# First MLP product: the weight sums behind both additions from PSUM, the low parts later, and a root one product later

## The chip, the cores and the metric

The kernel runs on one core of one Trainium2 chip. Its engines work side by side, each on its own queue of instructions: TensorE (PE in the profile; PEld are its weight loads) multiplies, VectorE (DVE), ScalarE (ACT) and GpSimd (POOL) do the rest, and SyncE (SP) starts transfers (DMA). They wait for one another through semaphores. SBUF is the memory that all engines work on, PSUM the banks that TensorE writes its products to. The metric is the time of one execution on the device in microseconds (us), less is better.

## The reference

Two sequences of 512 rows and 1024 columns go through two layers, a Fourier mixer with an MLP and an attention with an MLP:

```python
def sq_relu_mlp(h, w_up, w_down):
    a = jnp.maximum(h @ w_up, 0)
    return (a * a) @ w_down

def trunk(x, ...):
    for i in range(DEPTH):
        ...
        x = x + sq_relu_mlp(rms_norm(x, mlp_norm[i]), mlp_w_up[i], mlp_w_down[i])
    return rms_norm(x, final_norm)
```

`w_up` is 1024 x 4096 and `w_down` 4096 x 1024. Only `h @ w_up` of both layers, its squared ReLU, and the norm ahead of it bear on the change; the Fourier mixer, the attention and the second product are the same before and after.

## The kernel before

**Numbers.** Everything is float32. [...] A product is three matmuls for each 128 rows of depth: high by high, high by low, low by high. `halves` splits a 128 x 1024 tile and gives its two halves of 512 columns.

**The first MLP product** is one step of the Strassen-Winograd scheme over blocks: seven block products instead of eight. `h`, transposed and normed, gives four blocks, by depth (first or second 512) and by sequence (0 or 1); out of them `Blocks` makes b11, b21 (sequence 0), b12, b22 (sequence 1) and the sums t1 to t4. A `Pair` is two neighbouring tiles of 128 columns of `w_up`, of 512 KB each: `raw` holds a11 and a12 (the two halves of the depth), `r1` holds a21 and a22. From these VectorE makes four sums:

- `sums_23`, three instructions (L862, L863, L864): s3 = a11 - a21, then s1 = a21 + a22 in the place of a21, then s2 = s1 - a11. s2 and s3 share a tile `s` of the raw pool.
- `sum_4`: x4 = a12 - s2.

Then `split_23`, `split_1` and `split_4` make high and low parts: s2 and s3 with one cast and one subtraction of 1024 columns, s1 and a22 likewise, and x4 with 512 columns.

**The order in a pair.** `product` (L812) issues the 12 matmuls of one block product. `first` (b11) and `second` (b21) are the products of `raw`; `rest` does the other five in the order t2, t3, t1, t4, b22. In each layer the first pairs (`AHEADS`: 8 in layer 0, 6 in layer 1) have `first` and `second` done in a loop of their own, since they need sequence 0 alone, and are called early here; the later ones (`late`) have `first` ahead of `rest` and `second` within it, so that they have seven products and the early ones five. Layer 0 has 16 pairs, layer 1 has 14 and four tiles that are multiplied in the plain way (`Regular`).

`rest` accumulates in three banks, `ob`, `oc` and `od`, and VectorE adds their results:

- L885: u2 = t2's bank + b11's product, behind t2
- L889: u3 = bank `oc` + u2, behind t3. t4 goes on accumulating into `oc`, so its first matmul waits for this addition
- L900: u3 = bank `od` + u3, behind t1, then ReLU and square on ScalarE (`squares`, L827 and L828). b22 goes on accumulating into `od`, so it waits for this one
- L907: v = bank `oc` + u2, behind t4, then squares
- L914: bank `od` + u2, behind b22, then squares

Behind `rest`, `out` makes four subtractions on GpSimd (L922 to L925) for the second MLP product and seven transfers of the results to memory. While pair p is multiplied, the sums and the splits of pair p+1 (`nxt`) are made: they stand between the additions. The weights of pair p+2 are loaded behind `rest` of pair p (SP's queue).

**What sets the order.** In `rest` of the early pairs VectorE's order is the one that is written down (`manual_schedule` for DVE); the other engines' order there, and every order elsewhere, is found by the scheduler of the framework, which starts from the written order. `rest` of the last pair has VectorE's and SP's order by hand, and in layer 0 TensorE's too.

**The root.** The norm needs the inverse root of the mean square of each row of `x`. ScalarE squares the 8 tiles of a sequence (L157), GpSimd adds them up (L159), TensorE sums the columns (L165, 8 small matmuls by ones), and `rsqrt` makes the root with small instructions of VectorE and one or two of ScalarE. `spread` lets TensorE transpose the result to every partition (L173) and ScalarE copy it (L174). `Blocks.second` then norms sequence 1 (L212) and makes its blocks and sums, a part behind each of the early pairs from p = 4 on. `root(1)` is issued in the loop of the early pairs, behind `second` of p = 2, and `spread(1)` ahead of p = 3 in layer 0 and behind `second` of p = 3 in layer 1.

## Time and profile before

| | us |
|---|---|
| median of 3 runs | 1739.89 |
| lowest and highest | 1738.68, 1741.07 |
| the profiled execution, its own time | 1740.44 |
| its span, first to last instruction | 1738.6 |
| mean granted clock of TensorE | 0.992 |

The profile is one execution. Its stages, by stretches of the span with the busy time of TensorE in each:

| stretch, us | what runs there | TensorE busy, us |
|---|---|---|
| 0 to 160 | Fourier mixer, b11 and b21 of layer 0's early pairs | 130.82 |
| 160 to 290 | rest of the early pairs of layer 0 | 126.74 |
| 290 to 450 | late pairs of layer 0 | 159.46 |
| 450 to 870 | second product of layer 0 and the head of layer 1 | 414.47 |
| 870 to 1160 | rest of the attention, b11 and b21 of layer 1's early pairs | 287.32 |
| 1160 to 1260 | rest of the early pairs of layer 1 | 98.45 |
| 1260 to 1410 | late pairs of layer 1 | 150.00 |
| 1410 to 1738 | plain tiles, second product of layer 1, final norm | 318.07 |

The boundaries are rounded, so that a stretch holds a little of its neighbour. How to read it: a matmul's busy time runs to a modelled end and the next one overlaps it, so an idle time in a row is smaller than what the wait costs. A row of the timeline reads: start in us, length, engine, line, operation, output and inputs with their shapes, the number of instructions that the row stands for, and in brackets the idle time ahead of it with what ended it.

### The profile page before, as it was taken

Reading aid. Unit: us, or ns where it says so; the run is one execution under the profiler, and the core shown is the slowest. Engines: PE = TensorE matmul, PEld = TensorE weight load, DVE = VectorE, ACT = ScalarE, POOL = GpSimd, SP = SyncE. Lnnn points to the kernel's source line nnn. Section 1 sums busy time; section 2 is a strip of 40 time slices with the busy share of each in tenths; the row PEclk is TensorE's granted clock in tenths of the full one; section 3 lists DMA queues with packets and bytes.
Section 4 is the critical chain, followed back from the end, with each engine's and each line's share of the span. In section 5 each row is a group of like instructions: output and inputs, shape, how many; then the busy total and the mean of one; then the engine's idle time right before and its main releaser. Section 6 shows DMA issues by size and latency. Waiting matters only on the chain. (4 is left out here: it accounts for less than half of the span.)

```text
span 1738.6 us, 21980 instructions
## 1 busy us (share of the span) xinstructions
PE 1685.3 (97%) x7870; PEld 1396.4 (80%) x7870; DVE 1250.9 (72%) x1855; ACT 871.2 (50%) x1530; POOL 349.8 (20%) x308
## 2 busy tenths in 40 slices
PE   4999999999999999999999999999999999999997
PEld 4887788888788888788877888787788878888886
DVE  8768776555878879975578843697745479787865
ACT  6666444545433434546687724554544554344334
POOL 3330444222000000412234302104332200000004
PEclk9999999999999999999999999999999999999999
DMA  9823455448754545420100213225544487455322
GB/s 281 234 93 121 159 195 192 152 182 286 277 180 159 194 144 195 156 106 25 49 25 1 97 49 120 90 101 188 199 157 151 172 313 265 147 207 186 127 74 97
DMA packets 103893, 267.11 MB, mean 154 GB/s; under 512 B 10200, under 2 KB 10200, under 8 KB 103784
## 3 DMA queue, kind: packets, MB, share of 16 engines
q1 hardware_dynamic: 87624, 233.73, 37.5%
q10 hardware_dynamic: 14112, 25.70, 3.9%
q0 software_dynamic: 2048, 6.29, 1.9%
q8 instruction: 61, 1.00, 0.2%
q14 instruction: 48, 0.39, 0.1%
HBM read 190.70 MB, written 73.92 MB: 152 GB/s over the span
## 5 line engine op out<-in xcount | busy, mean ns | idle before, releaser
L812 PE MATMUL ps<-u,w 128*128 128x512 f32 x4704 | 1083.9, 391 | 9.5 <-DVE w L83 5.0
L812 PEld LDWEIGHTS ps<-u,w 128*128 128x128 f32 x4704 | 882.5, 188 | 202.7 <-DVE t L889 7.8
L82 ACT CAST w<-raw 128x1024 fp32r<-128x1024 f32 (+1 forms) x226 | 219.6, 982 | 428.2 <-PE ps L812 268.4
L83 DVE TENSOR_TENSOR w<-raw,w 128x1024 fp32r<-128x1024 f32 (+1 forms) x226 | 260.1, 1153 | 54.7 <-ACT w L82 54.3
L159 POOL TENSOR_TENSOR t<-t,t 128x512 f32<-128x512 f32 (+1 forms) x56 | 80.2, 1436 | 734.1 <-ACT t L157 678.5
L83 DVE TENSOR_TENSOR u<-u,u 128x1024 fp32r<-128x1024 f32 x133 | 163.0, 1254 | 23.9 <-ACT u L82 23.9
L82 ACT CAST u<-u 128x1024 fp32r<-128x1024 f32 x133 | 133.3, 1043 | 72.7 <-PE ps L812 47.5
L77 PE MATMUL ps<-u,u 128*128 128x512 f32 (+2 forms) x424 | 162.6, 385 | 1.7 <-DVE u L604 0.9
L78 PE MATMUL ps<-u,u 128*128 128x512 f32 (+2 forms) x424 | 157.6, 372 | 5.7 <-DVE u L83 5.6
L79 PE MATMUL ps<-u,u 128*128 128x512 f32 (+2 forms) x424 | 157.9, 372 | 2.0 <-POOL u L83 1.5
L1059 DVE TENSOR_TENSOR u<-ps,u 128x512 f32<-128x512 f32 x160 | 109.8, 689 | 57.1 <-PE ps L812 56.1
L812 PE MATMUL ps<-u,u 128*128 128x512 f32 x528 | 126.9, 390 | 2.6 <-DVE t L900 1.8
L922 POOL TENSOR_TENSOR u<-u 128x512 f32<-128x512 f32 x28 | 36.1, 1289 | 414.9 <-ACT u L828 414.9
L812 PEld LDWEIGHTS ps<-u,u 128*128 128x128 f32 x528 | 98.6, 188 | 25.5 <-issue 2.9
L78 PEld LDWEIGHTS ps<-u,u 128*128 128x128 f32 x424 | 82.9, 195 | 18.0 <-DVE u L83 7.8
L79 PEld LDWEIGHTS ps<-u,u 128*128 128x128 f32 x424 | 82.5, 195 | 15.9 <-POOL u L83 2.1
L77 PEld LDWEIGHTS ps<-u,u 128*128 128x128 f32 x424 | 83.0, 196 | 13.8 <-ACT u L82 1.8
L83 DVE TENSOR_TENSOR u<-ps,u 128x512 fp32r<-128x512 f32 (+4 forms) x126 | 76.5, 627 | 17.8 <-ACT u L82 16.5
L885 DVE TENSOR_TENSOR t<-ps,u 128x512 f32<-128x512 f32 x30 | 20.8, 692 | 91.4 <-PE ps L812 89.9
L82 ACT CAST u<-ps 128x512 fp32r<-128x512 f32 (+4 forms) x126 | 66.5, 542 | 24.9 <-PE ps L79 14.2
L795 DVE TENSOR_TENSOR u<-ps,u 128x512 f32<-128x512 f32 (+1 forms) x48 | 30.9, 645 | 64.7 <-PE ps L79 64.7
L827 ACT ACTIVATE t<-t 128x512 f32<-128x512 f32 x60 | 37.8, 631 | 56.1 <-DVE t L900 45.4
(225 smaller groups left out, 2007.8 us busy)
## 6 DMA issues: line engine op xcount, KB each, us to landing
raw<-w_up SPq DMA_DIRECT2D x82, 512.0 KB, 3.9
u<-spill_t SPq DMA_DIRECT2D x60, 512.0 KB, 6.0
raw<-w_sum SPq DMA_DIRECT2D x56, 512.0 KB, 3.7
u<-spill_b SPq DMA_DIRECT2D x45, 512.0 KB, 5.6
spill_t<-u SPq DMA_DIRECT2D x87, 256.0 KB, 2.0
spill_b<-t ACTq DMA_DIRECT2D x60, 256.0 KB, 2.0
raw<-w_row SPq DMA_DIRECT2D x28, 512.0 KB, 3.5
park<-u SPq DMA_DIRECT2D x24, 512.0 KB, 3.2
```

The costliest lines, as they stand in the source:

```text
L77: nc.tensor.matmul(out, lh, rh, start=first, stop=False)
L78: nc.tensor.matmul(out, lh, rl, start=False, stop=False)
L79: nc.tensor.matmul(out, ll, rh, start=False, stop=last)
L82: nc.scalar.copy(dst_hi, src)
L83: eng.tensor_sub(dst_lo, src, f32(dst_hi))
L159: nc.gpsimd.tensor_add(acc[q][:, :n], acc[q][:, :n], s[:, :n])
L795: nc.vector.tensor_add(x[:, :n], o[:, :n], x[:, :n])
L812: nc.tensor.matmul(o, w[x][:, sl], h[k][y], start=first and k + i == 0, stop=k == n - 1 and i == 2, skip_group_check=not first)
L827: nc.scalar.activation(t, src, AF.Relu)
L885: nc.vector.tensor_add(u2, ob, t[:, 0])
L922: eng.tensor_sub(t[:, 0], b12, b11)
L1059: nc.vector.tensor_add(x, o, x)
```

## The change

In `rest`, three things move in the written order, in both layers and all pairs but the last:

- `sums_23` of the next pair goes from between L885 and t3 to behind L889 (pair 0 had it there already).
- `split_23` goes from behind L889 to behind L900 and its squares.
- `sum_4` and `split_1` go from ahead of `v` to behind `v` and its squares.

In layer 0 alone (there `2 * np_ == NF`) two things move in the loop of the early pairs: `root(1)` from behind `second` of pair 2 to between `first` and `second` of pair 3, and `spread(1)` from ahead of pair 3 to ahead of pair 4. No instruction is added or removed. Behind the change the lines of `rest` from the second addition on stand two lower: L887 for L889, L896 for L900, and L920 to L923 for L922 to L925.

```diff
                 u2, u3, t = tm(), tm(), self.t
                 product(ob, self.s2, b("t2"))
                 nc.vector.tensor_add(u2, ob, t[:, 0])
-                if nxt and self.p > 0:
-                    nxt.sums_23()
                 product(oc, self.s3, b("t3"))
                 nc.vector.tensor_add(u3, oc, u2)
                 if self.late:
                     self.second()
                 if nxt:
-                    if self.p == 0:
-                        nxt.sums_23()
-                    nxt.split_23()
+                    nxt.sums_23()
                 if nxt and nxt.p >= ah:
                     nxt.split_row()
                 next(fill, None)
                 product(od, self.s1, b("t1"))
                 nc.vector.tensor_add(u3, od, u3)
                 squares(u3, u3)
+                if nxt:
+                    nxt.split_23()
                 product(oc, self.a22, b("t4"), False)
-                if nxt:
-                    nxt.sum_4()
-                    nxt.split_1()
                 next(fill, None)
                 v = tm()
                 nc.vector.tensor_add(v, oc, u2)
                 squares(v, v)
+                if nxt:
+                    nxt.sum_4()
+                    nxt.split_1()
                 next(fill, None)
                 if nxt:
                     nxt.split_4()
...
         for p in range(ah):
-            if 2 * np_ == NF and p == 3:
+            if 2 * np_ == NF and p == 4:
                 blocks.spread(1)
...
             pair.first()
+            if 2 * np_ == NF and p == 3:
+                blocks.root(1)
             if p > 0:
                 pair.second()
             if p == 1:
                 pairs[0].second()
-            if p == 2:
+            if p == 2 and 2 * np_ < NF:
                 blocks.root(1)
```

## The prediction

> **What bounds the kernel now.** I read the page first: its span, and the share of it that each engine is busy.

> ```profile
> span 1738.6 us, 21980 instructions
> PE 1685.3 (97%) x7870; PEld 1396.4 (80%) x7870; DVE 1250.9 (72%) x1855; ACT 871.2 (50%) x1530; POOL 349.8 (20%) x308
> raw<-w_up SPq DMA_DIRECT2D x82, 512.0 KB, 3.9
> ```

> TensorE is busy 97% of the span, and the change removes no matmul. So it can only shorten or lengthen TensorE's waits. The waits of TensorE by releaser (total, times, longest) say which of them the edited lines can reach.

> ```profile
> PE ps L812 <- DVE t L889: 2.8, 2, 1.9
> PE ps L165 <- POOL t L159: 2.6, 3, 1.5
> PE ps L812 <- DVE t L900: 1.8, 3, 0.6
> ```

> L889 is the second addition from PSUM in `rest`, L900 the third, L165 the column sums in `root`. These totals are too small: a gap counts only past the modelled end of a matmul. TensorE's timeline shows what hides. I take the third to fifth pair of layer 0; the rows of 12 are the last product of a pair (b22), the rows of 48 the next pair's first four.

> ```profile
> 190.24 2.88 PE L812 MATMUL ps<-u,u 128*128 128x512 f32 x12
> 204.07 2.88 PE L812 MATMUL ps<-u,u 128*128 128x512 f32 x12
> 206.79 11.34 PE L812 MATMUL ps<-u,w 128*128 128x512 f32 x48
> 217.96 2.88 PE L812 MATMUL ps<-u,u 128*128 128x512 f32 x12
> ```

> A product of 12 takes 206.79 - 204.07 = 2.72 us, 0.227 per matmul, so five take 13.61; but a pair takes 217.96 - 204.07 = 13.89. The missing 0.28 us is a short wait in every pair, before t4, which accumulates onto the bank that L889 reads. VectorE, GpSimd (POOL) and ScalarE in such a pair, whose t2 starts at 206.79:

> ```profile
> 206.99 0.69 DVE L914 TENSOR_TENSOR u<-ps,t 128x512 f32<-128x512 f32 x1 [0.49 <-PE ps L812]
> 209.77 0.69 DVE L885 TENSOR_TENSOR t<-ps,u 128x512 f32<-128x512 f32 x1 [2.08 <-PE ps L812]
> 210.37 0.68 DVE L862 TENSOR_TENSOR raw<-raw,raw 128x512 f32<-128x512 f32 x1
> 211.09 1.67 DVE L863 TENSOR_TENSOR raw<-raw 128x512 f32<-128x512 f32 x1
> 212.79 1.66 DVE L864 TENSOR_TENSOR raw<-raw,raw 128x512 f32<-128x512 f32 x1
> 214.38 0.68 DVE L889 TENSOR_TENSOR t<-ps,t 128x512 f32<-128x512 f32 x1
> 215.62 1.23 DVE L83 TENSOR_TENSOR w<-raw,w 128x1024 fp32r<-128x1024 f32 x1 [0.57 <-ACT w L82]
> 209.14 1.29 POOL L922 TENSOR_TENSOR u<-u 128x512 f32<-128x512 f32 x1 [7.42 <-ACT u L828]
> 210.51 1.70 POOL L923 TENSOR_TENSOR u<-t,u 128x512 f32<-128x512 f32 x1
> 212.17 1.73 POOL L924 TENSOR_TENSOR u<-t,u 128x512 f32<-128x512 f32 x1
> 213.87 1.74 POOL L925 TENSOR_TENSOR t<-t,u 128x512 f32<-128x512 f32 x1
> 214.54 2.00 ACT L82 CAST w<-raw 128x1024 fp32r<-128x1024 f32 x2 [5.53 <-DVE raw L864]
> ```

> The sums L863 and L864 take 1.67 instead of 0.69 us: each ends 0.55 after a POOL subtraction ends, and each subtraction ends 1.15 after a sum. Two-operand instructions on SBUF of these engines take turns. L889, which reads PSUM, takes 0.68 beside a running POOL. It is late because it stands behind the sums.

> **The change, part 1: sums behind both additions.** No instruction is added. Three sums (L862 to L864) go behind the second addition, which then ends at 5.44 + 0.26 + 0.69 = 6.39 us from the pair's start (an addition starts 0.26 behind its product: 209.77 against 206.79 + 2.72), before t4 at 8.16. The wait of 0.28 goes, but something else is late: the third addition now stands behind the sums, and b22 waits for it at 10.89.

> Let POOL start its four subtractions at 3.94. They run 3.94 to 5.23 and 5.31 to 6.60. L862, ready at 6.31, ends 0.55 later, at 7.15; the third subtraction at 8.30, L863 at 8.85, the fourth at 10.00, L864 at 10.55. The third addition runs 10.46 to 11.15 (successive starts overlap by 0.09, as 209.77 + 0.69 and 210.37 show), and b22 starts at 11.21 instead of 10.89: 0.32, and 0.11 for the weight load restarting, together 0.43 us.

> Then the cast runs 10.64 to 11.69 (0.09 behind L864, two of them 2.00) and the low part to 12.94, before the next t2 needs it at 14.04. v's addition starts at 12.85, the fourth sum 13.45, the low part of the raw pair 14.06, that of x4 15.23, and t0's addition 15.84 to 16.53. L914 ended at 207.68 and POOL began at 209.14, two squares and 1.46 later; so POOL starts at 17.99, which is 3.95 in the next pair of 14.04. The ring closes: **0.43 against 0.28 now.** Where ScalarE makes the square of v before the cast of x4 (in the changed order the first three pairs of layer 0), POOL starts 0.2 later and the wait is 0.52 + 0.11 = 0.63.

> The first pairs and the last one ahead of the long ones have their own rows.

> ```profile
> 171.33 2.20 PE L812 MATMUL ps<-u,w 128*128 128x512 f32 x9
> 174.28 2.36 PE L812 MATMUL ps<-u,w 128*128 128x512 f32 x9 [0.75 <-ACT w L82]
> 187.38 2.79 PE L812 MATMUL ps<-u,w 128*128 128x512 f32 x11 [1.89 <-DVE t L889]
> 274.29 0.93 PE L812 MATMUL ps<-u,u 128*128 128x512 f32 x3 [0.61 <-DVE t L900]
> 1175.54 1.66 PE L812 MATMUL ps<-u,w 128*128 128x512 f32 x6 [0.94 <-DVE t L889]
> 172.46 0.69 DVE L864 TENSOR_TENSOR raw<-raw,raw 128x512 f32<-128x512 f32 x1
> ```

> To each bracket 0.16 is added, because a matmul's record lasts 0.39 while the next is due after 0.227, and some 0.1 for the restart. Pair 0 of layer 0 loses 0.75 + 0.16 + 0.11 = 1.02, pair 1 loses 1.89 + 0.16 + 0.11 = 2.16, pair 7 loses 0.85; with six short waits layer 0 loses 1.02 + 2.16 + 6 x 0.28 + 0.85 = 5.7. Layer 1: 1.21 + 4 x 0.28 + 0.85 = 3.2. Of pair 0's nine matmuls from 174.28, all belong to pair 1 and cover part of a wait; the changed order puts b22 of pair 0 first.

> After: in pair 0 I hang VectorE's order on the product ends; L864 ends about 173.7 (now 173.15, because the second addition waits for t3 ahead of a low part), b22 is due at 173.37 and waits for the addition that ends at 174.3: 1.0 + 0.11. POOL then starts at 4.2 in pair 1. Pairs 1 to 3 cost 0.63 each, 4 to 6 0.43. In pair 7 the low part of the next row stands ahead of the third addition too: one cast more on ScalarE in pair 6 puts POOL at 4.43, L864 ends at 11.0, the low part after the last subtraction at 12.2, the addition at 12.8, b22 waits 1.95 + 0.11 = 2.06. Layer 0: 1.1 + 1.9 + 1.3 + 2.1 = 6.4. Layer 1 starts with POOL at 2.6 and no wait in three pairs, then 0.53, 0.43 and 2.06: 3.0. **Part 1: 9.4 - 8.9 = +0.5 us.**

> Bounds: below, if the sums never meet POOL, only pair 0 waits, and 9.4 falls to 1.1, a gain of 7.8. Above, if all three sums wait a whole turn (1.67 each, as L863), the third addition ends at 11.95 and b22 waits 1.23 in each pair: 11 pairs x 1.23 and twice 2.9 make 20.4 with pair 0's 1.1, a loss of 11.5. I take the ring, because it closes on the rows' own durations.

> **What moves at no cost.** The low parts go behind the squares: the next t2 needs them at 14.04 and they end at 12.94, a cover of 1.1 us. The raw buffers come free some 2 us later, so two loads per pair start later on SP; they land in 3.9 us and are needed 6.3 us into the next pair but one. The long pairs (seven products, 19.05 us) have the final addition at about 12.85 against b22 at 13.6: no wait, as now.

> **Part 2: the root of sequence 1.** It issues column sums on TensorE, five small VectorE and two ScalarE instructions, no DMA; its spread four transposes and a copy.

> ```profile
> 120.79 1.09 PE L812 MATMUL ps<-u,w 128*128 128x512 f32 x4
> 123.40 1.26 PE L165 MATMUL ps<-ones,t 128*128 128x2 f32 x8 [1.52 <-POOL t L159]
> 121.61 1.03 ACT L82 CAST w<-raw 128x1024 fp32r<-128x1024 f32 x1
> 120.69:124.10 3.41, 1.19 (x6) 0.62 (x4) 1.00 0.69 275
> 124.10:127.52 3.42, 3.00 (x7) 2.49 (x8) 0.50 0.00 0
> 185.55:188.96 3.41, 1.58 (x7) 1.32 (x8) 1.00 0.42 162
> 135.52 4.63 DVE L212 TENSOR_TENSOR u<-u,t 128x1024 f32<-128x1024 f32 x4 [0.43 <-ACT t L174]
> 142.85 1.23 DVE L83 TENSOR_TENSOR w<-raw,w 128x1024 fp32r<-128x1024 f32 x1 [1.57 <-ACT w L82]
> ```

> TensorE waits 1.52 us for the last square's addition on POOL. The last three rows with a colon are windows of L812 alone (TensorE's busy time, its loads', the granted clock, DMA): behind a window with 1.19 us of full matmuls in 3.41 (35%) the clock is 0.50 for 3.42 us; behind one with 1.58 (46%) it stays at 1.00. At half clock seven matmuls take 3.0 us, 1.4 to 1.5 more than at full clock.

> In the changed order only two matmuls of pair 3 come ahead of the sums. They need the cast that ends at 122.64, run 122.7 to 123.15, and the sums start at 123.40 as now. That is 0.45 us of work inside the wait. It also lifts the window to 1.64 us (48%), above the one that kept its clock. **Part 2: -0.45 - 1.49 = -1.9 us.** Bounds: 0, if the cast is late, and -2.0. The norms (L212) move behind one more low part; VectorE is idle for 1.57 before 142.85, so this is covered; without the cover it costs 1.2.

> [...]

> **Sum.** The profiled execution took 1740.44 us for its span of 1738.6. 1740.44 + 0.5 - 1.9 = **1739.0 us**; the median of the runs is 1739.89, 0.55 lower than the profiled one. I hold to the former.

> **Rivals.**
> A, no meeting: if POOL starts at 2.6 to 3.3 in every pair, as at the head of layer 1, the waits of pairs 1 to 6 and of layer 1 fall away (1.9 + 1.3 + 1.0) and the two long ones to today's 0.85 (2.4): 1739.0 - 6.6 = 1732.4. For it: the ring has slack of 0.3 only. Against: low parts now stand ahead of t0's addition, and 15.84 against today's 14.1 follows from fixed durations.
> B, slower, the ring slips: if POOL starts past 4.9, the three sums meet three subtractions. One mechanism, at b22: 1.23 us in nine pairs (six of layer 0, three of layer 1) instead of 3.2 + 1.0, so 1739.0 + 11.1 - 4.2 = 1745.9. For it: a delay feeds itself from pair to pair, and pair 6 gets half of it from one cast. Against: it needs 1 us beyond the ring's 3.94.
> C, the half clock stays: the wait at the column sums shrinks, but the clock falls all the same. 1740.5. For it: 48% is close to 46%, and the window's phase can differ in another execution. Against: two windows with less than 40% fell, the one with 46% did not.

> ```profile
> 728.27:731.68 3.41, 1.27 (x6) 1.00 0.97 386
> 731.68:735.09 3.41, 3.41 (x10) 0.50 0.71 246
> ```

> **How the numbers follow.** Forecast 0.45, A 0.25, B 0.18, C 0.12. No change within 0.2% (3.5 us, about what a measurement of this kernel can tell from none) is 1736.4 to 1743.4 around the median. The forecast's own range, 1736 to 1741.5, lies in it but for its low end; C lies in it. So faster: A's 0.25 and 0.09 of the forecast, 0.34; slower: B's 0.18 and 0.03 for both parts near their upper bounds, 0.21; same 0.45. The range reaches through A's price to 1732.0 and most of the way to B's, 1744.5, leaving out some 0.18.

> **What would show it.** Right: no wait on the second addition any more, waits of b22 on the third one (0.1 to 0.5 us in the records, about 2 in pair 7 and in pair 5 of layer 1), POOL's first subtraction about 3.9 us behind t2's start, sums of 0.84 and 1.67 us; clock 1.00 after the column sums. Wrong: sums of 0.69 each (A), all three at 1.67 (B), a window at 0.50 near 125 us (C), or a wait of t2 for a low part, which my cover of 1.1 us excludes.

## The result and the profile after

The changed kernel took 1743.69 us in the median of 20 runs (1739.92 to 1747.32), the kernel before 1740.2 us (1736.25 to 1742.0, 20 runs): 1.0020 of it, with a 95% interval of 1.0013 to 1.0027, so 3.5 us slower. The prediction was 1739.0, about one microsecond faster. The profiled execution took 1744.79 us, 4.35 more than the one before, its span 3.7 more. First the top of the page of the changed kernel; then a line of its TensorE waits (total, times, longest), and TensorE at the column sums.

```profile
span 1742.3 us, 22000 instructions
PE 1686.2 (97%) x7870; PEld 1398.0 (80%) x7870; DVE 1258.0 (72%) x1855; ACT 864.9 (50%) x1530; POOL 345.3 (20%) x308
```

```profile
PE ps L812 <- DVE t L896: 8.4, 12, 2.4
```

```profile
122.83 0.73 PE L812 MATMUL ps<-u,w 128*128 128x512 f32 x2 [0.79 <-ACT w L82]
123.56 1.05 PE L165 MATMUL ps<-ones,t 128*128 128x2 f32 x8
```

At the column sums (L165) the wait of 1.52 us is gone; the two matmuls ahead of them wait 0.79 us for their cast instead (ScalarE's cast, L82, makes the high part of an operand, VectorE's subtraction, L83, its low part). The wait for the second addition (now L887) is gone from the list. In its place stands the third one, L896, 12 times. TensorE's timeline shows where; the rows with `u,u` are b22. First layer 0, then layer 1.

```profile
173.34 2.98 PE L812 MATMUL ps<-u,u 128*128 128x512 f32 x12 [1.04 <-DVE t L896]
187.46 2.98 PE L812 MATMUL ps<-u,u 128*128 128x512 f32 x12 [0.25 <-DVE t L896]
201.68 3.01 PE L812 MATMUL ps<-u,u 128*128 128x512 f32 x12 [0.36 <-DVE t L896]
215.92 3.01 PE L812 MATMUL ps<-u,u 128*128 128x512 f32 x12 [0.35 <-DVE t L896]
218.77 11.04 PE L812 MATMUL ps<-u,w 128*128 128x512 f32 x48
230.00 2.97 PE L812 MATMUL ps<-u,u 128*128 128x512 f32 x12 [0.19 <-DVE t L896]
244.08 2.98 PE L812 MATMUL ps<-u,u 128*128 128x512 f32 x12 [0.24 <-DVE t L896]
258.17 3.00 PE L812 MATMUL ps<-u,u 128*128 128x512 f32 x12 [0.23 <-DVE t L896]
261.01 11.04 PE L812 MATMUL ps<-u,w 128*128 128x512 f32 x48
274.39 3.88 PE L812 MATMUL ps<-u,u 128*128 128x512 f32 x9 [2.34 <-DVE t L896]
```

```profile
1206.37 2.97 PE L812 MATMUL ps<-u,u 128*128 128x512 f32 x12 [0.23 <-DVE t L896]
1220.46 2.98 PE L812 MATMUL ps<-u,u 128*128 128x512 f32 x12 [0.24 <-DVE t L896]
1236.72 4.58 PE L812 MATMUL ps<-u,u 128*128 128x512 f32 x12 [2.40 <-DVE t L896]
```

From b22 to b22 a pair takes 244.08 - 230.00 = 14.08 us, where the prediction had 14.04 and the kernel before 13.89. The ring of GpSimd and VectorE is there as it was worked out. VectorE and GpSimd in the pair that starts at 218.77:

```profile
224.46 0.69 DVE L887 TENSOR_TENSOR t<-ps,t 128x512 f32<-128x512 f32 x1 [2.03 <-PE ps L812]
225.07 0.78 DVE L862 TENSOR_TENSOR raw<-raw,raw 128x512 f32<-128x512 f32 x1
225.88 1.66 DVE L863 TENSOR_TENSOR raw<-raw 128x512 f32<-128x512 f32 x1
227.58 1.67 DVE L864 TENSOR_TENSOR raw<-raw,raw 128x512 f32<-128x512 f32 x1
229.17 0.68 DVE L896 TENSOR_TENSOR t<-ps,t 128x512 f32<-128x512 f32 x1
222.64 1.29 POOL L920 TENSOR_TENSOR u<-u 128x512 f32<-128x512 f32 x1 [8.02 <-ACT u L828]
```

GpSimd starts 222.64 - 218.77 = 3.87 us into the pair (forecast 3.94), the third addition 10.40 (10.46), b22 11.23 (11.21). So the steady pairs are not where the forecast failed. The last early pair of each layer waits 2.34 and 2.40, and its b22 is then long by itself: 4.58 us for 12 matmuls in layer 1 instead of 2.88. In the traces of before and after, every change of the granted clock lies a whole number of 3.413 us from every other (124.10, 127.52, 731.68 and 735.09 are four in the one, 274.38, 277.80, 1236.94 and 1240.35 in the other); a window is one such step, and where the clock does not change at its boundary, the boundary is counted in these steps from a change. The windows of L812 at these two waits and behind them (TensorE's busy time, its loads', granted clock, DMA share, GB/s):

```profile
270.97:274.38 3.41, 1.08 (x5) 0.58 (x4) 1.00 0.46 165
274.38:277.80 3.42, 3.40 (x8) 2.74 (x9) 0.50 0.90 307
1233.53:1236.94 3.41, 1.00 (x5) 0.57 (x4) 1.00 0.57 172
1236.94:1240.35 3.41, 3.41 (x9) 2.63 (x9) 0.50 0.88 311
```

Behind each long wait the clock is 0.50 for one window. It lets 8 matmuls start where a full one fits 15 (3.41 / 0.227): seven lost, 7 x 0.227 = 1.6 us, for each of the two.

### The profile page after: what moved, and what is told of

Same layout as the page of the kernel before. It is cut to its first block, busy times and chain, and to the rows that moved or that the text cites. A ratio compares the mean times of both kernels' runs of the same rounds, so it can differ in the third digit from the quotient of the medians.

```text
span 1742.3 us, 22000 instructions
## 1 busy us (share of the span) xinstructions
PE 1686.2 (97%) x7870; PEld 1398.0 (80%) x7870; DVE 1258.0 (72%) x1855; ACT 864.9 (50%) x1530; POOL 345.3 (20%) x308
## 5 line engine op out<-in xcount | busy, mean ns | idle before, releaser
L812 PE MATMUL ps<-u,w 128*128 128x512 f32 x4704 | 1079.1, 390 | 7.0 <-DVE w L83 5.0
L812 PEld LDWEIGHTS ps<-u,w 128*128 128x128 f32 x4704 | 882.4, 188 | 195.5 <-DVE w L83 7.4
L82 ACT CAST w<-raw 128x1024 fp32r<-128x1024 f32 (+1 forms) x226 | 220.9, 981 | 452.0 <-PE ps L812 275.3
L83 DVE TENSOR_TENSOR w<-raw,w 128x1024 fp32r<-128x1024 f32 (+1 forms) x226 | 262.8, 1165 | 74.6 <-ACT w L82 74.1
L159 POOL TENSOR_TENSOR t<-t,t 128x512 f32<-128x512 f32 (+1 forms) x56 | 80.3, 1437 | 734.8 <-ACT t L157 679.1
L83 DVE TENSOR_TENSOR u<-u,u 128x1024 fp32r<-128x1024 f32 x133 | 163.0, 1252 | 23.7 <-ACT u L82 23.0
L82 ACT CAST u<-u 128x1024 fp32r<-128x1024 f32 x133 | 133.1, 1042 | 67.9 <-PE ps L812 48.0
L812 PE MATMUL ps<-u,u 128*128 128x512 f32 x528 | 131.1, 399 | 9.5 <-DVE t L896 8.4
L812 PEld LDWEIGHTS ps<-u,u 128*128 128x128 f32 x528 | 100.2, 192 | 36.3 <-issue 7.9
L920 POOL TENSOR_TENSOR u<-u 128x512 f32<-128x512 f32 x28 | 36.6, 1307 | 423.8 <-ACT u L828 423.8
L83 DVE TENSOR_TENSOR u<-ps,u 128x512 fp32r<-128x512 f32 (+4 forms) x126 | 76.6, 627 | 17.6 <-ACT u L82 16.2
L82 ACT CAST u<-ps 128x512 fp32r<-128x512 f32 (+4 forms) x126 | 66.5, 542 | 24.8 <-PE ps L79 14.0
L885 DVE TENSOR_TENSOR t<-ps,u 128x512 f32<-128x512 f32 x30 | 20.7, 690 | 69.3 <-PE ps L812 64.0
L77 PE MATMUL ps<-u,w 128*128 128x512 f32 (+2 forms) x192 | 65.0, 338 | 0.0
## 6 DMA issues: line engine op xcount, KB each, us to landing
raw<-w_up SPq DMA_DIRECT2D x82, 512.0 KB, 4.5
u<-spill_t SPq DMA_DIRECT2D x60, 512.0 KB, 5.8
raw<-w_sum SPq DMA_DIRECT2D x56, 512.0 KB, 3.7
u<-spill_b SPq DMA_DIRECT2D x45, 512.0 KB, 6.1
raw<-w_row SPq DMA_DIRECT2D x28, 512.0 KB, 3.6
park<-u SPq DMA_DIRECT2D x24, 512.0 KB, 3.1
```

Of the source, the lines that this page charges most:

```text
L77: nc.tensor.matmul(out, lh, rh, start=first, stop=False)
L82: nc.scalar.copy(dst_hi, src)
L83: eng.tensor_sub(dst_lo, src, f32(dst_hi))
L159: nc.gpsimd.tensor_add(acc[q][:, :n], acc[q][:, :n], s[:, :n])
L812: nc.tensor.matmul(o, w[x][:, sl], h[k][y], start=first and k + i == 0, stop=k == n - 1 and i == 2, skip_group_check=not first)
L885: nc.vector.tensor_add(u2, ob, t[:, 0])
```

## The experiments

Theory: the extra time lies in the two long waits and in the half clock behind them, and the ring's short waits are as forecast. Of the root's move the first run still expected the forecast's 1.9 us. Rivals: the time is spread over all pairs; the half clock has nothing to do with the waits; the sums alone, not the row's low part, make the long wait. "Before" in the comparisons is the kernel before, run again beside each group of experiments. The edits are shown in part; "..." marks what is left out.

### The two parts alone

The root alone, with `rest` as before:

```diff
-            if 2 * np_ == NF and p == 3:
+            if 2 * np_ == NF and p == 4:
                 blocks.spread(1)
...
+            if 2 * np_ == NF and p == 3:
+                blocks.root(1)
...
-            if p == 2:
+            if p == 2 and 2 * np_ < NF:
                 blocks.root(1)
```

> Only the move of root(1) and spread(1) is made, rest() is that of before. My theory (the wait of 1.52 us and the half clock behind it both go, as the trace after shows at 123 to 128 us): 1.9 us less than before, some 1738.3, no window at 0.50 near 125 us. Rival (the half clock near 125 us hangs on the execution and not on the wait): 0.4 us less at most, 1739.8, and a window at 0.50 there.

Measured: 1740.11 against 1739.55, ratio 0.9999 (0.9991 to 1.0008). The theory's 1.9 us are not there, and the rival's half clock is. The windows around the column sums of this kernel, and behind them the one of the changed kernel in its own profile:

```profile
119.35:122.76 3.41, 1.51 (x5) 0.61 (x5) 1.00 0.52 213
122.76:126.17 3.41, 3.41 (x9) 2.62 (x8) 0.50 0.00 0
```

```profile
120.78:124.20 3.42, 2.00 (x8) 0.99 (x6) 1.00 0.74 296
124.20:127.61 3.41, 2.97 (x13) 2.44 (x14) 1.00 0.00 0
```

It is the same order of instructions at the column sums in both. In one execution the window's boundary cuts the stretch with little work, and 2.00 us of full matmuls (512 columns each) fall into the window; in the other 1.51 do, and the clock falls. Of the eleven profiles of this study with the later root, five have a window at 0.50 behind the column sums; of the three with the earlier one, two. These are too few to tell the two orders apart.

`rest` alone, with the root as before:

```diff
-                if nxt and self.p > 0:
-                    nxt.sums_23()
...
                 if nxt:
-                    if self.p == 0:
-                        nxt.sums_23()
-                    nxt.split_23()
+                    nxt.sums_23()
...
+                if nxt:
+                    nxt.split_23()
```

(and `sum_4` and `split_1` behind `v`, as in the change).

> Only the order in rest() is changed, the root stays where it was before. Theory (two long waits of b22, in pair 7 of layer 0 and pair 5 of layer 1, each of some 2.5 us, each with a window at half clock behind it that costs 1.7 us): 1740.2 + 5.4 = 1745.6, with windows at 0.50 near 125, 275 and 1237 us. Rival (the extra time is spread over all pairs, by slower sums or later loads): also above before, but without the windows at 275 and 1237 us.

Measured: 1744.54 against 1739.55, ratio 1.0024 (1.0014 to 1.0033), close to the theory's 1745.6. The whole loss is in `rest`. The profiled execution (1745.57) is a poor witness for the size, since 3.2 us of its loss against the profile before come late: a wait of 2.41 us in layer 1's second product (at 1433, for L1057) with a half clock of its own, where the other profiles have between nothing and 1.38. Both long waits are there, but only one brought the half clock in the profile:

```profile
270.39:273.80 3.41, 1.60 (x8) 0.98 (x6) 1.00 0.41 157
273.80:277.22 3.42, 2.82 (x12) 2.36 (x13) 1.00 0.95 320
1232.95:1236.36 3.41, 1.20 (x5) 1.04 (x6) 1.00 0.67 207
1236.36:1239.78 3.42, 3.42 (x9) 2.65 (x9) 0.50 0.86 320
```

The first wait lies across a boundary (273.80) and leaves 1.60 us of work in its window; the second lies within one and leaves 1.20. So whether the half clock came went with where the windows lay, and that differed between the two executions: one begins at 274.38 in the profile of the changed kernel and at 273.80 here (counted back from the change at 1236.36), while b22 of pair 0 starts at 173.34 in both.

### The long wait and its clock

The low part of the next pair's row behind the third addition, in the last early pair:

```diff
-                if nxt and nxt.p >= ah:
+                if nxt and self.p >= ah:
                     nxt.split_row()
...
                 squares(u3, u3)
+                if nxt and self.p == ah - 1:
+                    nxt.split_row()
```

> As after, but in the last early pair of each layer the low part of the next pair's row goes behind the third addition and its squares. Theory (it is the row's low part, which waits for GpSimd's last subtraction, that holds the third addition): both long waits fall to the 0.4 us of the other pairs and the half clock behind them goes: twice 2.5 + 1.7 - 0.4 = 7.6 us less than after, 1736.1, and 4 us less than before. Rival 1 (the sums hold it): the waits stay at 2 us, 1743. Rival 2 (the row comes too late for the next pair's first product): the wait moves there, 1741 or more.

Measured: 1736.42 against 1739.55, ratio 0.9981 (0.9972 to 0.9990). The time is the theory's 1736.1, the rows are so only in part. The wait of pair 7 is 0.09 us in the record, but pair 5 of layer 1 keeps 1.23, and here the rival has it right: the sums alone hold the addition. GpSimd starts 4.91 us into this pair (1224.31 against t2 at 1219.40), and all three sums take a full turn:

```profile
1225.70 1.82 DVE L862 TENSOR_TENSOR raw<-raw,raw 128x512 f32<-128x512 f32 x1
1227.55 1.67 DVE L863 TENSOR_TENSOR raw<-raw 128x512 f32<-128x512 f32 x1
1229.26 1.66 DVE L864 TENSOR_TENSOR raw<-raw,raw 128x512 f32<-128x512 f32 x1
```

This is the prediction's upper bound, three sums at a whole turn each, in one pair of the 14.

Four matmuls more inside each long wait, into a bank that nobody reads:

```diff
+                if self.p == ah - 1:
+                    z, x = ps(), b("t4")[0][0]
+                    for i in range(4):
+                        nc.tensor.matmul(z, self.a22[0][:, :128], x, start=True, stop=True)
                 product(od, self.s4, b("b22"), False)
```

> As after, with four more matmuls in the last early pair of each layer, ahead of b22, into a bank that nobody reads: 0.9 us of work inside each long wait, nothing else is changed. Theory (the half clock comes from a window of 3.41 us with too little work in it; with the fill about 56% instead of 30%): the waits end when they did, the windows at 0.50 near 275 and 1237 us go, 3.4 us less than after, 1740.3. Rival (the half clock is not caused by the idle time): windows stay, 1743.7 as after.

Measured: 1742.07 against 1739.55, ratio 1.0016 (1.0007 to 1.0025): no window at 0.50 behind either wait, but 1.6 us less than the changed kernel's 1743.69 rather than 3.4. Since that compares runs taken at different times, both kernels ran again unchanged, side by side:

> The changed kernel once more, beside e10_fill4_again on the same chip. Theory (a window of 3.41 us in which full matmuls fill under some 45% is followed by one at half clock, and the windows' phase against the program differs from execution to execution: an idle stretch of 2.4 us takes 1.88 us of one window in (3.41 - 2.4 + 2 x 0.52) / 3.41 = 0.60 of the phases): each long wait brings the half clock in 6 executions of 10, and its mean price is 0.6 x 1.6 = 1.0 us. Median 3.5 above before. Rival (every execution pays it): the two windows stand in this profile too, and it is 3.3 us slower than e10_fill4_again.

> The kernel of e4_fill4 once more, beside e9_after_again. Theory: 2 x 1.0 = 2.0 us faster than e9_after_again (0.9988 of it), the waits at b22 end when they did, no window at 0.50 near 274 and 1235 us. Rival (clock and waits have nothing to do with each other): the two kernels agree within 0.5 us.

Measured: 1743.26 for the changed kernel and 1741.01 with the fill, against 1739.35: ratios 1.0019 (1.0010 to 1.0028) and 1.0011 (1.0003 to 1.0020). The medians differ by 2.25 us, near the theory's 2.0. The two sets of 11 times differ by 1.9 us in the mean, with a 95% interval of some 0.4 to 3.3: there is a difference, but its size is loose, and the rival's 3.3 lies at the edge. The profiles agree with the theory. The changed kernel again has a window at 0.50 behind both waits; with the fill TensorE's timeline and windows read:

```profile
271.14 1.07 PE L914 MATMUL ps<-u,w 128*128 128x512 f32 x4
273.62 2.97 PE L812 MATMUL ps<-u,u 128*128 128x512 f32 x12 [1.42 <-DVE t L896]
```

```profile
270.47:273.88 3.41, 1.99 (x9) 1.00 0.56 186
273.88:277.30 3.42, 3.42 (x16) 1.00 0.93 343
```

The wait ends as it did, for the same addition, with work of no use in it, and the clock stays at 1.00. Without the fill, five of six long waits in the three profiles that have them (this kernel twice, `rest` alone once) were followed by 0.50; with it none of four.

### What the sums wait for

GpSimd's four subtractions left out in the early pairs (this kernel leaves out a part of the result, and only its time is read):

```diff
                 p = self.p
+                if p < ah:
+                    for op, x in (("b11", b11), ("b21", b21), ("b22", b22), ("t1", b12), ("t2", b12),
+                                  ("t3", b12), ("t4", b12)):
+                        put(op, p, x, queue)
+                    return
```

> As after, but the four subtractions of GpSimd behind each early pair are left out (t1 to t4 are stored from another tile, so the result is not the reference's); VectorE's order is that of after. Theory (the sums are late because they take turns with these subtractions): all sums take 0.69 us, b22 waits in no pair but the first, the long waits go as well and with them the half clock: 1743.7 - 5.5 (layer 0) - 3.7 (layer 1) - 2 (clock) = 1732.5. Rival (three sums and a row's low part are too long for the 4.5 us by themselves): pairs 1 to 6 lose their 0.4 us, the long waits stay over 1 us: 1738.

Measured: 1730.15 against 1740.55, ratio 0.9944 (0.9931 to 0.9958). VectorE's order is that of the change, and pair 7 now reads:

```profile
266.92 0.69 DVE L864 TENSOR_TENSOR raw<-raw,raw 128x512 f32<-128x512 f32 x1
267.52 1.22 DVE L83 TENSOR_TENSOR w<-raw,w 128x1024 fp32r<-128x1024 f32 x1
268.66 0.68 DVE L896 TENSOR_TENSOR t<-ps,t 128x512 f32<-128x512 f32 x1
```

Three sums and the row's low part end in time for b22 when nothing runs beside them; no early pair but the first waits. The rival, too much work on VectorE by itself, falls.

The sums moved, the low parts not:

```diff
                 if nxt:
                     nxt.sums_23()
+                    nxt.split_23()
...
                 squares(u3, u3)
-                if nxt:
-                    nxt.split_23()
                 product(oc, self.a22, b("t4"), False)
+                if nxt:
+                    nxt.sum_4()
+                    nxt.split_1()
...
                 squares(v, v)
-                if nxt:
-                    nxt.sum_4()
-                    nxt.split_1()
```

> As after, but the low parts stand where they stood before: split_23 right behind the sums, sum_4 and split_1 ahead of v. Theory (the third addition now stands behind the sums and a cast and a low part of 1.2 us, while GpSimd starts 1.5 us earlier): b22 waits 1 to 2 us in each early pair, 1748 to 1756. Rival (GpSimd's earlier start makes the sums short enough that nothing waits): 1735 to 1741.

Measured: 1751.69 against 1740.55, ratio 1.0067 (1.0054 to 1.0079). The third addition stands behind the low part, which stands behind a cast; the low part and the addition, then TensorE:

```profile
189.98 1.23 DVE L83 TENSOR_TENSOR w<-raw,w 128x1024 fp32r<-128x1024 f32 x1 [1.17 <-ACT w L82]
191.12 0.68 DVE L897 TENSOR_TENSOR t<-ps,t 128x512 f32<-128x512 f32 x1
```

```profile
190.00 2.38 PE L812 MATMUL ps<-u,w 128*128 128x512 f32 x9 [1.08 <-ACT w L82]
```

Here TensorE's order has nine matmuls of the next pair ahead of b22, and they wait for that cast, some 1.1 us in the record in each of pairs 1 to 6 of layer 0.

The low parts moved, the sums not:

```diff
+                if nxt and self.p > 0:
+                    nxt.sums_23()
                 product(oc, self.s3, b("t3"))
...
-                if nxt:
+                if nxt and self.p == 0:
                     nxt.sums_23()
```

> As after, but the sums stand where they stood before, ahead of the second addition; only the low parts come later. Theory (t4 waits for the second addition as before, some 0.3 us a pair, as the sums meet GpSimd; the third addition has no sum ahead of it, and the row's low part in the last early pair stands behind fewer of them): 1738 to 1741, no wait over 1.5 us at b22. Rival (GpSimd's later start, which comes with the later low parts, is what makes the sums slow): t4 waits over 1 us in each pair, 1748 or more.

Measured: 1741.31 against 1740.55, ratio 1.0003 (0.9994 to 1.0012), just past the theory's upper end of 1741. A pair takes 14.06 us (b22 starts at 200.44 and 214.50), with the wait at t4. So the moved sums need the moved low parts, and the two together are worse than the low parts alone: the wait goes from t4 to b22, and grows in the last early pair, where the row's low part stands behind the sums.

### A version without the wait

As with the later row, and the third sum behind the third addition too, in the early pairs:

```diff
                 nc.vector.tensor_add(u3, od, u3)
+                if nxt and self.p < ah:
+                    nxt.sum_2()
                 squares(u3, u3)
+                if nxt and self.p == ah - 1:
+                    nxt.split_row()
```

where `sum_2` is L864, taken out of `sums_23`; everywhere else it is called right behind `sums_23`.

> As e3_row_later, and the third sum (L864) also goes behind the third addition in the early pairs. Theory (in each pair the third addition waits for the last sum alone, some 0.4 us; in pair 5 of layer 1, where GpSimd starts early enough to meet all three sums, 1.4 us): of the 6.2 us that b22 still waits in e3_row_later about 5 go, 1736.4 - 5 = 1731.4. Rival (the low part of s2 and s3 comes 0.6 us later and the next t2 waits for it, since without the waits a pair is 13.6 us long): the wait moves to t2, 1734 to 1737.

Measured: 1729.06 against 1740.55, ratio 0.9945 (0.9932 to 0.9957): faster than both kernels. TensorE, with b22 in the middle row:

```profile
215.81 11.04 PE L812 MATMUL ps<-u,w 128*128 128x512 f32 x48
226.69 2.88 PE L812 MATMUL ps<-u,u 128*128 128x512 f32 x12
229.41 11.10 PE L812 MATMUL ps<-u,w 128*128 128x512 f32 x48
```

229.41 - 215.81 = 13.60 us for a pair: five products of 2.72, and no wait. The rival, a late low part for t2, did not come. Run once more, and beside it with the root where it was before the change:

> The kernel of e5_sum2_later once more. Theory: 0.9945 of before again, some 11 us less, with no wait over 0.4 us in the early pairs.

> The kernel of e5_sum2_later with root(1) and spread(1) where they were before the change, beside e12_best_again. Theory (the later root saves 0.45 us at the column sums and gives it back, since VectorE's norms and low parts all run later and the first pair waits 0.7 us longer; the half clock near 125 us comes in some executions of both): within 1 us of e12_best_again. Rival (the prediction's step: the root's move is worth 1.9 us): 1.9 us slower than e12_best_again.

Measured against 1739.35: 1732.77, ratio 0.9957 (0.9944 to 0.9970), with the later root, and 1730.62, ratio 0.9946 (0.9934 to 0.9958), with the earlier one. The version repeats its gain, if smaller than the first time (the interval holds the first ratio of 0.9945). The two lie 2.15 us apart, more than the 1 us that was expected, and to the disadvantage of the later root. Nothing speaks for the later root; with the root alone, whose interval ends at 0.9991, a gain of 1.9 us (0.0011) from it is excluded.

## Why the prediction was wrong, point by point

The forecast was 1.4 us less than the profiled execution before, and 3.5 us more were measured. Three terms make up these 4.9 us: the waits were 1.4 us longer than forecast, the half clock behind the two long ones, which the prediction does not have, took about 2, and of the root's 1.9 us the times show nothing. The three come to about 5, and without the new half clocks the other two would still make a loss.

**The ring of sums and subtractions: right.** The pair of 14.04 was 14.08, GpSimd's start 3.94 was 3.87, and b22's wait of 0.43 was 0.46 to 0.51 in pairs 4 to 6 (the bracket and 0.27, as the prediction counted it) and 0.52 to 0.63 in pairs 1 to 3 against 0.63. Layer 1 had no wait in its first three pairs, as forecast. That the meeting with GpSimd makes the sums long is shown by leaving the subtractions out: L863 and L864 take 0.69 us each there, and 1.66 and 1.67 in the changed kernel.

**The long waits: too small.** The prediction had 2.06 us each; they were 2.34 + 0.27 = 2.61 and 2.67. It put GpSimd's start in pair 7 at 4.43, and it was 266.18 - 261.01 = 5.17. Its first and last subtraction there, VectorE, and a cast of ScalarE ahead of them:

```profile
266.18 1.29 POOL L920 TENSOR_TENSOR u<-u 128x512 f32<-128x512 f32 x1 [9.30 <-ACT u L828]
270.83 1.73 POOL L923 TENSOR_TENSOR t<-t,u 128x512 f32<-128x512 f32 x1
269.75 1.67 DVE L864 TENSOR_TENSOR raw<-raw,raw 128x512 f32<-128x512 f32 x1
271.34 2.31 DVE L83 TENSOR_TENSOR w<-raw,w 128x1024 fp32r<-128x1024 f32 x1
273.57 0.68 DVE L896 TENSOR_TENSOR t<-ps,t 128x512 f32<-128x512 f32 x1
261.36 1.05 ACT L82 CAST w<-raw 128x1024 fp32r<-128x1024 f32 x1 [0.79 <-DMA raw<-w_up]
```

The last row is the one cast more that the prediction reckoned with, that of the next pair's row. What it did not reckon with is the bracket: the cast stands 0.79 us until its load has landed, and the squares and subtractions behind it stand too. "What moves at no cost" had the loads in time. In layer 1 this cast waits 0.85 us and GpSimd starts at 5.24; in the kernel with the later row it waits 0.52 there and GpSimd starts at 4.91, the same 0.33 earlier. So the wait for the load sets how late GpSimd starts, though no run takes it away alone.

The row's low part takes 2.31 us instead of 1.22 and ends 1.09 behind the last subtraction's end at 272.56. The prediction had it behind that subtraction too, but ending 12.2 us into the pair; it was 271.34 + 2.31 - 261.01 = 12.64. The eleven waits sum to 1.31 (pair 0) + 1.77 + 1.47 + 2.61 + 3.68 (layer 1) = 10.84, against 9.4 forecast and 8.9 before: in waits part 1 is +1.94 where it was to be +0.5.

**The clock behind the long waits: left out, and this is the step that failed.** The prediction used the windows to say that the wait at the column sums brings the half clock, and then forecast two new waits of 2.06 us without putting them through the same rows; the cost of a half clock behind them was put at nothing, with no reason given. A wait of 2.06 is 2.06 - 0.27 = 1.79 us idle in the record and leaves 3.41 - 1.79 = 1.62 us of work in a window that holds it, 47%, or 41% with the "about 2" that its signs name: around the 46% that kept its clock, and no safe margin. The waits that came, some 0.6 us longer, left 1.08 and 1.00, some 30%, less than the 35 and 37% that fell. Whether the half clock would have come behind waits of 2.06 no run shows. In the profile it cost 2 x 1.6 = 3.2 us; in the mean over executions the fill puts it at about 2 (1.6 and 2.25 between medians).

**The clock at the column sums: taken as fixed.** The prediction counted 1.49 us for a half clock that would go, and gave 0.12 to its staying. It did go in the profile after, and stayed in others with the same order. It went with where the windows lay, which rival C named: the window at the column sums held 2.00 us of full matmuls in the profile after and 1.51 in that of the root alone, and 0.50 stood behind the second only. Where they lay differed between profiles (boundaries at 274.38 and 273.80 beside the same work).

**The root's 0.45 us: given back.** TensorE waits 0.79 us ahead of the two matmuls, where the column sums waited 1.52 before, and the column sums follow at 123.56 without a wait. But pair 0 waits 1.04 in the record with the later root, and 0.37 with `rest` changed alone. The cover that the prediction named, 1.57 us of idle VectorE ahead of 142.85, does not reach that far: VectorE's work behind the norms runs later up to the first pair. In the root alone, too, pair 0 waits longer, 1.43 instead of 0.75. From the same matmul near 110 us (the 601st in the record) to b22 of pair 0 it is 62.4 to 62.6 us in the three profiles of the changed kernel and the fill that have the later root and no half clock at the column sums, 64.0 to 64.2 in three with the half clock (the later row, the fill, no subtractions), and 63.28 with the earlier root and the half clock (`rest` alone). So where the half clock comes in both, the later root is some 0.8 us slower up to there, not 0.45 faster.

**The sum.** In the profiled execution: +1.94 for the waits, +3.2 for two half clocks, -1.48 for the one at the column sums, some -0.3 for the wait there (two matmuls of 0.45, with the sums' start 0.16 later), together +3.4 of the 3.7 us by which the spans differ. Over the runs, with 2.0 for the new half clocks and nothing for the root's, 1.94 + 2.0 - 0.3 = 3.64 against 3.5 measured; that it agrees so closely is in part luck, since the 2.0 is loose. Rival B got the sign, but not for its reason: of the orders with all three sums behind the second addition and ahead of the third, only one pair, and only in the kernel with the later row, had all three at a whole turn. In pair 7 GpSimd did start past rival B's 4.9, but there the first sum met the end of the first subtraction and took 0.70.

## What to carry to other kernels

A wait that a change creates needs the same test as the wait that it removes: if the profile shows a slower clock behind a short wait, ask for it behind every new one. Here it stood behind a wait of 1.52 us before the change, and behind five of six long ones in the three profiles of the changed `rest`. Ask also by how much a wait may outgrow its forecast (2.06 us was forecast, 2.61 and 2.67 came). In `rest` alone only one of the two long waits had the half clock behind it, so a gain that consists of a clock window gone is worth its mean over executions and not the one seen. And when work is moved behind the instruction that is late, ask which instruction stands behind it now: here an order that lets both additions go ahead of the last sum and the row's low part gained 7 to 11 us (two sets of runs), where the change only passed the wait on.

## What was not expected of the hardware

```profile
118.79:122.20 3.41, 1.50 (x7) 0.89 (x5) 1.00 0.76 298
122.20:125.61 3.41, 2.83 (x12) 2.36 (x13) 1.00 0.00 0
```
